# A chunk recurrence put on the diagonal corners of TensorE's array and scheduled first

## The chip, the cores and the metric

The kernel runs on one core of a Trainium2 chip. The metric is the device time of one execution in microseconds (us); three executions of the kernel before took 3286.41, 3289.52 and 3295.87 us, median 3289.52. The core has five engines that each work through a queue of their own in order: TensorE (PE in the profile; its weight loads are listed apart as PEld), VectorE (DVE), ScalarE (ACT), GpSimd (POOL) and SyncE (SP, which here issues DMAs).

## The reference

One decoder block on 2048 tokens of 1024 channels. A projection `w_in` feeds two mixers: eight heads of an RWKV-7 recurrence (64 channels each) and four heads of differential attention. Their outputs are concatenated, projected by `w_out`, added to the input, and followed by a gated MLP with a short causal convolution. The change touches the recurrence only:

```python
def step(state, inp):                       # per head, state is 64 x 64
    r_t, w_t, k_t, v_t, kk_t, a_t = inp
    sa = jnp.einsum('bhvk,bhk->bhv', state, -kk_t)
    state = (state * w_t[:, :, None, :]
             + sa[..., None] * (kk_t * a_t)[:, :, None, :]
             + v_t[..., None] * k_t[:, :, None, :])
    return state, jnp.einsum('bhvk,bhk->bhv', state, r_t)
_, y = lax.scan(step, s0, seq_major)        # 2048 steps
```

## The kernel before

The program is a list of instructions that a scheduler orders: each engine takes, of what is ready by the scheduler's own timing, the instruction that was written first, and buffers come from pools with a fixed number of slots per tag. So the order in which the Python code emits work is its priority.

The recurrence is done in 32 chunks of 64 tokens, two chunks to a group (16 groups, class `Rwkv`). For each group there are four steps. `prepare` (L383) makes the decayed keys and queries AR and BK for all eight heads (two heads per 128 partitions), multiplies them into the matrices M of each head (L470, tiles se and so for even and odd heads), transposes values into `sav` and keys into `bkt`, and sends the diagonal 32 x 32 blocks of M through DRAM (adr) into tile ab. `invert` (L502) inverts those blocks on VectorE by 31 pairs of dependent instructions (L515, L517) and sends the result X through DRAM (xdr) back into M, bdx and x1t, all by SP's queue. `join` (L535) makes the blocks off the diagonal. `scan` (L557) carries the state S over the two chunks:

- rp (L570, L573): what the old state and the chunk's own values give, for all heads, in PSUM partitions 0 to 63; ScalarE copies it to rsb (L575);
- sp (L578): rsb times the inverse, copied by ScalarE into the lower half of `sav` (L579);
- up (L583): the change of the state; VectorE adds it (L588) and applies the decay (L591), once for each half of the partitions;
- yp (L594, L597): the output, from the old state and from `sav`, added to ybv (L600).

The state is kept as 128 x 128 per pair of heads with zeros off the diagonal blocks. In `sav` the 64 upper partitions hold the values, the 64 lower ones the result of sp, for even and odd heads alike. A float32 matmul counts as two passes in the profile. `post` (L605) normalises and gates the last group's output in between.

`block_kernel` interleaves: first the blocks of the projection (tile pp, lines L99 to L101 in helper `mm3`, 24 matmuls for 512 tokens, in two halves of the tokens, the second named pp1_...), then the 64 attention units (4 heads of 16 query blocks; tiles sp at L775 to L778, tp at L813, op at L819, ot at L838) with the steps of the recurrence between them, at most up to unit 44 (`SPREAD`); from unit 40 (`ALONE`) attention uses the recurrence's PSUM slots. Then come the output projection (tile po) and the MLP (fp, dn). The recurrence's PSUM tiles have two slots in tag ra (prepare) and two in rc (join, scan, post).

Of the kernel before, what the change touches and what calls it, by code (L numbers as in the profile page):

```python
# [8 lines left out]
F32 = mybir.dt.float32  # L9
# [45 lines left out]
def rms_rstd(nc, cx, pool, src, n, eps, name, junk):  # L55
    """[128,1] = (mean(src^2) + eps)^-0.5 over the free axis; src is a list of APs."""
# [10 lines left out]
def norm_rows(nc, cx, pool, dst, src, gain, t):  # L67
    """dst = rms-normalised rows of src times gain; both SBUF [128, 1024], tokens x channels."""
# [9 lines left out]
def transpose_split(nc, cx, ps, xn, xh, xl, t, tag, bufs):  # L78
    """xn: SBUF [128, 1024] tokens x channels; writes tokens t*128.. of xh/xl, lists of [128, 8, GRP] tiles."""
# [16 lines left out]
def mm3(nc, out, lh, ll, rh, rl, n):  # L96
    """out = sum over kb of (lh+ll)^T (rh+rl) without ll*rl; callables give the operands of kb."""
# [28 lines left out]
class Proj:  # L126
    """Projections of x by w_in, one half of the tokens at a time."""
# [25 lines left out]
    def load(self, t, first=None):  # L153
        """128 tokens of normalised x, transposed and split; the second half's rows come from prepare()."""
# [38 lines left out]
    def pair(self, a, b, w=None):  # L193
        """Two blocks, the first tokens of both before the last."""
# [5 lines left out]
    def start(self, first):  # L200
        """Loads the first half and does its first two blocks."""
# [20 lines left out]
    def shift(self, cb, g, pp):  # L222
        """Token shift of an RWKV block."""
# [49 lines left out]
def rwkv_consts(tc, nc, cx, I):  # L273
# [95 lines left out]
class Rwkv:  # L369
    """Time mixing, 128 tokens at a time, in four stages per group."""  # L370
# [12 lines left out]
    def prepare(self, g):  # L383
# [71 lines left out]
        tt(BK[:, :, :, 0, :], c4(b2), c4(ip), op=ALU.mult)  # L455
        tt(BK[:, :, :, 1, :], c4(kp), c4(ip), op=ALU.mult)
# [697 lines left out]
```

## Time and profile before

| | |
|---|---|
| median of three runs | 3289.52 us |
| span of the profiled execution | 3295.9 us (the slowest run reads 3295.87 us, so nothing measurable lies around the span) |
| TensorE | 3178.5 us busy, 96% of the span |
| VectorE, ScalarE, GpSimd | 58%, 35%, 10% |
| granted TensorE clock, mean | 0.964 of full speed |
| chain that ended last | PE 82%, DVE 4%, DMA 4% |

Busy is the time in which an engine works on at least one instruction. The granted clock is a mean over two levels, 1.2 and 2.4 GHz, so 0.96 says that 8% of the time was spent at the lower one. By the tiles the span has four stages: projection with the first groups of the recurrence (to 943 us), attention with the rest of it (to about 1440), attention alone (to 1636), output projection and MLP (to the end).

### The profile page before, as it was taken

The page shows a single profiled execution, that of the slowest core. Times are in us where ns is not written, and L with a number is a line of the kernel's source. Part 1 is how long each engine was busy: PE and PEld are TensorE (multiplying, and loading weights), DVE is VectorE, ACT ScalarE, POOL GpSimd, SP SyncE. Part 2 cuts the span into 40 slices and gives each one's busy share as a digit, 9 for nine tenths or more (in the row PEclk, how much of TensorE's full clock was granted, in tenths as well). Part 3 has the DMA queues.
Part 4 walks back from the last instruction along what each step waited for, and adds up shares of the span by engine and source line. Part 5 has one row for each costly group of instructions (what it writes and reads, how often), then busy time and mean ns, then how long its engine had stood idle before and what let it go on. Part 6 is the DMA issues. An engine that isn't in the chain of part 4 may idle for free.

```text
span 3295.9 us, 44432 instructions
## 1 busy us (share of the span) xinstructions
PE 3178.5 (96%) x16579; PEld 2594.6 (79%) x16579; DVE 1923.8 (58%) x4898; ACT 1167.9 (35%) x2268; POOL 332.6 (10%) x441
## 2 busy tenths in 40 slices
PE   8999999999989989898999999999999999999997
PEld 6887777777777767677888888888888788888886
DVE  5246555455457868568655455555556655555556
ACT  4233322232225555467633422222223422222223
POOL 3001000010022232233200000000000000000002
PEclk9999999999878999899999999999999999999999
DMA  5355523234372252415244311111112411111112
GB/s 159 96 158 165 146 87 99 82 82 104 91 123 59 53 104 58 72 53 136 78 141 166 122 51 52 45 45 56 48 45 82 155 52 45 45 54 49 52 33 83
DMA packets 361177, 282.30 MB, mean 86 GB/s; under 512 B 95823, under 2 KB 307378, under 8 KB 360962
## 3 DMA queue, kind: packets, MB, share of 16 engines
q1 hardware_dynamic: 333874, 247.11, 25.9%
q0 software_dynamic: 24784, 28.16, 4.6%
q10 hardware_dynamic: 2304, 4.20, 0.4%
q8 instruction: 131, 2.15, 0.3%
q14 instruction: 84, 0.69, 0.1%
HBM read 204.72 MB, written 73.88 MB: 85 GB/s over the span
## 4 chain that ended last, share of the span: by engine, by line
PE 82%; DVE 4%; DMA 4%; issue 1%; ACT 1%; SPq 1%; POOL 0%; ACTq 0%; DVEq 0%; POOLq 0%
PE fp L99 10%; PE fp L101 9%; PE fp L100 9%; PE dn L100 5%; PE dn L99 5%; PE dn L101 5%; PE pp L99 4%; PE pp L100 4%; PE pp L101 4%; PE op L819 3%; PE po L99 2%; PE po L101 2%; PE sp L775 2%; PE po L100 2%; PE rp L573 2%; PE rp L570 2%
## 5 line engine op out<-in xcount | busy, mean ns | idle before, releaser
L1001 DVE TENSOR_TENSOR acc<-dn,acc 128x512 f32<-128x512 f32 x320 | 211.6, 688 | 224.3 <-PE dn L101 222.0
L99 PE MATMUL fp<-f1h,uh 128*128 128x512 f32 x704 | 275.8, 392 | 3.7 <-DVE fcarry L966 3.7
L100 PE MATMUL fp<-f1l,uh 128*128 128x512 f32 x704 | 275.2, 391 | 0.0
L101 PE MATMUL fp<-f1h,ul 128*128 128x512 f32 x704 | 275.1, 391 | 0.0
L100 PE MATMUL dn<-dl,gh 128*128 128x512 f32 x704 | 274.5, 390 | 0.0
L99 PE MATMUL fp<-f0h,uh 128*128 128x512 f32 x704 | 274.2, 389 | 0.0
L101 PE MATMUL fp<-f0h,ul 128*128 128x512 f32 x704 | 274.1, 389 | 0.0
L100 PE MATMUL fp<-f0l,uh 128*128 128x512 f32 x704 | 274.0, 389 | 0.0
L99 PE MATMUL dn<-dh,gh 128*128 128x512 f32 x704 | 271.7, 390 | 1.9 <-DVE acc L1001 1.9
L101 PE MATMUL dn<-dh,gl 128*128 128x512 f32 x704 | 263.4, 390 | 0.0
L780 DVE TENSOR_SCALAR_CACHE_REDUCE E<-sp 128x512 f32<-128x512 f32 (+3 forms) x320 | 188.4, 606 | 82.8 <-PE sp L778 45.7
L93 DVE TENSOR_TENSOR ul<-ur,uh 128x1024 fp32r<-128x1024 f32 x88 | 107.7, 1225 | 186.9 <-ACT uh L92 186.9
L962 DVE SCALAR_TENSOR_TENSOR u<-fp,cvA,u 128x511 f32<-128x511 f32 x176 | 131.4, 747 | 119.8 <-ACT u L960 119.8
L819 PE MATMUL op<-V,at 128*128 128x128 f32 x1088 | 163.6, 295 | 26.3 <-ACT at L815 25.3
L92 ACT CAST dh<-dr 128x1024 fp32r<-128x1024 f32 x44 | 44.4, 1047 | 386.6 <-PE dn L101 383.9
L819 PEld LDWEIGHTS op<-V,at 128*128 128x128 f32 x1088 | 146.1, 204 | 41.3 <-ACT at L815 32.7
L99 PE MATMUL pp<-x1h,wh 128*128 128x512 f32 x416 | 174.5, 419 | 0.0
L101 PE MATMUL pp<-x1h,wl 128*128 128x512 f32 x416 | 172.6, 415 | 0.0
L515 DVE TENSOR_TENSOR xtmp<-X,ab 128x60 f32<-128x60 f32 (+24 forms) x496 | 110.2, 222 | 105.9 <-DMA ab<-adr 76.2
L100 PE MATMUL pp<-x1l,wh 128*128 128x512 f32 x416 | 171.6, 412 | 0.0
L100 PE MATMUL pp<-x0l,wh 128*128 128x512 f32 x416 | 167.9, 404 | 0.0
L99 PE MATMUL pp<-x0h,wh 128*128 128x512 f32 x416 | 167.3, 403 | 0.1
(302 smaller groups left out, 7013.2 us busy)
## 6 DMA issues: line engine op xcount, KB each, us to landing
ur<-in_w_up SPq DMA_DIRECT2D x88, 512.0 KB
wr<-in_w_in SPq DMA_DIRECT2D x52, 512.0 KB
dr<-in_w_down SPq DMA_DIRECT2D x44, 512.0 KB
rw<-e SPq DMA_DIRECT2D x56, 256.0 KB
x<-in_x SPq DMA_DIRECT2D x16, 512.0 KB
qq<-e SPq DMA_DIRECT2D x64, 128.0 KB
kk<-e SPq DMA_DIRECT2D x64, 128.0 KB
ab<-adr SPq DMA_DIRECT2D x64, 128.0 KB
```

The source lines that it names most:

```text
L93: nc.vector.tensor_tensor(wl, wr, wh.bitcast(F32), op=ALU.subtract)
L99: nc.tensor.matmul(out, lh(kb), rh(kb), start=(kb == 0), stop=False)
L100: nc.tensor.matmul(out, lh(kb), rl(kb), start=False, stop=False)
L101: nc.tensor.matmul(out, ll(kb), rh(kb), start=False, stop=(kb == n - 1))
L515: tt(tv, X[:, 0:n, j:j + 1].broadcast_to([P, n, w]), ab[:, j:j + 1, j + 1:32].broadcast_to([P, n, w]), op=ALU.mult)
L570: nc.tensor.matmul(rp[0:64, 2 * hb:2 * hb + 2, :], AR[:, hb, c, 0, :], S[:, hb, :], start=True, stop=False)
L573: nc.tensor.matmul(rp[0:64, h, :], M[64:128, c, h, 0:64], sav[64:128, c, h, :], start=False, stop=(e == 1))
L775: nc.tensor.matmul(sp[:, 0:n], qa[:, c, qs], ka[:, c, 0:n], start=True, stop=False)
L780: nc.vector.tensor_scalar(e[ch * GRP // EW][:, eo:eo + n], sp[:, 0:n], -1.0, None, op0=ALU.mult, op1=ALU.min, accum_out=mx[:, ch:ch + 1])
L819: nc.tensor.matmul(op, at[:, q, :], v[:, q, :], start=(kb == 0), stop=(kb == qb))
L962: stt(u[:, 1:GRP], pp[:, 0:GRP - 1], w1(b), u[:, 1:GRP], op0=ALU.mult, op1=ALU.add)
L1001: nc.vector.tensor_tensor(acc[:, t, ds_], po, acc[:, t, ds_], op=ALU.add)
```

## The change

The even head of a pair now lives on partitions 0 to 63 and the odd head on 64 to 127 in everything that the recurrence reads: M, the two halves of `sav` and `bkt` change places for odd heads. The state shrinks to 64 columns per pair. rp, sp and the state's part of yp become eight matmuls each of 64 x 64 (rows 0 to 63 to columns 0 to 63 of the array for even heads, 64 to 127 to 64 to 127 for odd), even and odd in turn. The part of rp that comes from the chunk's own values is made in `prepare` (tile wp, copied to kv); VectorE adds rp to it. up and the other part of yp keep all 128 rows with 64 columns, even and odd in turn. The scan's instructions are emitted under `tc.high_priority()`, which puts them ahead of all else that is ready. The DMAs of adr and of M are split by even and odd heads. (Doc strings are removed as well; lines after them keep their places, later lines move.)

```diff
-        s = c.tile([P, 4, P], F32, name=f"state{i}")
+        s = c.tile([P, 4, 64], F32, name=f"state{i}")
...
-        tt(BK[:, :, :, 0, :], c4(b2), c4(ip), op=ALU.mult)
-        tt(BK[:, :, :, 1, :], c4(kp), c4(ip), op=ALU.mult)
+        for e in range(2):
+            rs = slice(64 * e, 64 * e + 64)
+            tt(BK[rs, :, :, e, :], c4(b2[rs]), c4(ip[rs]), op=ALU.mult)
+            tt(BK[rs, :, :, 1 - e, :], c4(kp[rs]), c4(ip[rs]), op=ALU.mult)
...
         for d in range(2):
-            ds_ = slice(32 * d, 32 * d + 32)
-            nc.sync.dma_start(adr[d].rearrange("b j i -> j b i"), M[ds_, :, :, ds_].rearrange("j c h i -> j (c h) i"))
+            for e in range(2):
+                r = 64 * e + 32 * d
+                nc.sync.dma_start(adr[d].rearrange("(b e) j i -> e j b i", e=2)[e],
+                                  M[r:r + 32, :, :, 32 * d:32 * d + 32].rearrange("j c (b e) i -> e j (c b) i", e=2)[e])
...
+        kv = T([P, NC, 4, 64], "kv", SB)
+        wp = U([P, NC, 4, 64], "wp")
+        for c in range(NC):
+            for hb in range(4):
+                for e in range(2):
+                    h, ks = 2 * hb + e, slice(64 * (1 - e), 64 * (1 - e) + 64)
+                    nc.tensor.matmul(wp[64 * e:64 * e + 64, c, hb, :], M[ks, c, h, 0:64], sav[ks, c, h, :],
+                                     start=True, stop=True)
+        nc.scalar.copy(kv, wp)
...
         for d in range(2):
-            ds_ = slice(32 * d, 32 * d + 32)
-            nc.sync.dma_start(M[ds_, :, :, ds_].rearrange("j c h i -> j (c h) i"),
-                              xdr[d].rearrange("b m s i -> (m s) b i"))
+            for e in range(2):
+                r = 64 * e + 32 * d
+                nc.sync.dma_start(M[r:r + 32, :, :, 32 * d:32 * d + 32].rearrange("j c (b e) i -> e j (c b) i", e=2)[e],
+                                  xdr[d].rearrange("(b e) m s i -> e (m s) b i", e=2)[e])
...
-            rp = U([P, 8, 64], f"rp{c}")
-            for hb in range(4):
-                nc.tensor.matmul(rp[0:64, 2 * hb:2 * hb + 2, :], AR[:, hb, c, 0, :], S[:, hb, :], start=True, stop=False)
+            with tc.high_priority():
+                rp = U([P, 4, 64], f"rp{c}")
+                for hb, e, h, rs in both:
+                    nc.tensor.matmul(rp[rs, hb, :], AR[rs, hb, c, 0, :], S[rs, hb, :], start=True, stop=True)
+                rsb = kv[:, c]
+                tt(rsb, rp, rsb, op=ALU.add)
+                sp = U([P, 4, 64], f"sp{c}")
+                for hb, e, h, rs in both:
+                    nc.tensor.matmul(sp[rs, hb, :], M[rs, c, h, 0:64], rsb[rs, hb, :], start=True, stop=True)
+                sv = sav[:, c].rearrange("p (b e) x -> e p b x", e=2)
                 for e in range(2):
-                    h = 2 * hb + e
-                    nc.tensor.matmul(rp[0:64, h, :], M[64:128, c, h, 0:64], sav[64:128, c, h, :], start=False, stop=(e == 1))
-            rsb = T([P, 8, 64], "rsb")
-            nc.scalar.copy(rsb[0:64], rp[0:64])
-            sp = U([P, 8, 64], f"sp{c}")
-            for h in range(8):
-                nc.tensor.matmul(sp[0:64, h, :], M[0:64, c, h, 0:64], rsb[0:64, h, :], start=True, stop=True)
-            nc.scalar.copy(sav[0:64, c], sp[0:64])
+                    rs = slice(64 * e, 64 * e + 64)
+                    nc.scalar.copy(sv[e][rs], sp[rs])
             next(post, None)
...
+            with tc.high_priority():
+                yp = U([P, 4, 64], f"yp{c}")
+                for hb, e, h, rs in both:
+                    nc.tensor.matmul(yp[rs, hb, :], S[rs, hb, :], AR[rs, hb, c, 1, :], start=(hb == 0), stop=False)
+                up = U([P, 4, 64], f"up{c}")
+                for hb, e, h, rs in both:
+                    nc.tensor.matmul(up[rs, hb, :], bkt[:, c, 64 * h:64 * h + 64], sav[:, c, h, :], start=True, stop=True)
+                st = T([P, 4, 64], "st")
+                tt(st, S, up, op=ALU.add)
+                tt(Sn, st, pc[:, :, c:c + 1].broadcast_to([P, 4, 64]), op=ALU.mult)
+                for hb, e, h, rs in both:
+                    nc.tensor.matmul(yp[rs, hb, :], sav[:, c, h, :], M[:, c, h, 64:128], start=False, stop=(hb == 3))
+                yv = ybv[:, :, 64 * c:64 * c + 64]
+                tt(yv, yp, yv, op=ALU.add)
```

The order of instructions moves with it. On TensorE, where the state is read for group 4's chunk 0 during the projection (rp0_4 is rp of chunk 0 of group 4, xp_4 its join, vt and bt group 5's transposes, pp the projection), there stood before:

```order
L101 MATMUL pp1_13_1_5090<-x1h1_3044,wl1_13_5055 128x512
L545 MATMUL xp_4_5223<-ident_84,x1t_4_5221 128x32 x4
L570 MATMUL rp0_4_5241<-state0_588,AR_4_4100 64x128
L573 MATMUL rp0_4_5241<-sav_4_4340,M_4_4305 64x64 x2
L570 MATMUL rp0_4_5241<-state0_588,AR_4_4100 64x128
L488 MATMUL vt_5_5123<-ident_84,vv_5_4875 128x128 x4
L496 MATMUL bt0_5_5131<-ident_84,BK_5_4883 128x128 x4
L573 MATMUL rp0_4_5241<-sav_4_4340,M_4_4305 64x64 x2
```

In the changed kernel (se1_5 and so1_5 are group 5's products, L590 is rp's new line, L560 the join's) there stands:

```order
L101 MATMUL pp1_13_1_5247<-x1h1_3129,wl1_13_5212 128x512
L560 MATMUL xp_4_5403<-ident_84,x1t_4_5401 128x32
L590 MATMUL rp0_4_5422<-state0_588,AR_4_4221 64x64 x8
L560 MATMUL xp_4_5403<-ident_84,x1t_4_5401 128x32 x3
L472 MATMUL se1_5_5185<-AR_5_5035,BK_5_5036 128x128 x2
L472 MATMUL so1_5_5186<-AR_5_5035,BK_5_5036 128x128 x2
```

The eight pieces of rp (five are shown), with other groups' work between them, have become one piece of eight equal matmuls.

At the end of the projection on TensorE (pp1_25_1 is its last tile) there stood before, from the last projection matmul on:

```order
L101 MATMUL pp1_25_1_7829<-x1h1_3044,wl1_25_7798 128x512
L470 MATMUL se0_10_7660<-AR_10_7522,BK_10_7523 128x128 x4
L545 MATMUL xp_9_7900<-ident_84,x1t_9_7793 128x32 x4
L570 MATMUL rp0_9_7939<-state0_588,AR_9_7026 64x128
L573 MATMUL rp0_9_7939<-sav_9_7188,M_9_7091 64x64 x2
```

In the changed kernel (up1_7 and gp_6 belong to the scan of group 7 and the post of group 6, n2_9 to the prepare of group 9):

```order
L101 MATMUL pp1_25_1_8169<-x1h1_3129,wl1_25_8138 128x512
L607 MATMUL up1_7_7266<-sav_7_6345,bkt_7_6355 64x64 x8
L644 MATMUL gp_6_7287<-sg_6_5630,gup_533 128x128 x4
L366 MATMUL n2_9_7322<-rT0_556,sel_555 128x128 x4
L560 MATMUL xp_8_7597<-ident_84,x1t_8_7595 128x32 x4
L590 MATMUL rp0_8_7688<-state0_588,AR_8_6769 64x64 x8
```

The first rp after the projection is that of group 9 before and that of group 8 now: one group more of the recurrence stands among the attention units. At the other end, the last rp (group 15, chunk 1) stood behind the output of head 2's query block 2 (unit 34) before, and stands behind that of its query block 7 (unit 39) now.

On SP's queue, among the attention units, the return of group 12's inverse (xdr_12) into M, bdx and x1t stood so before (ab_13 and X_13 are loads for the next group's inverse):

```order
L481 DMA ab_13_10221<-adr_13_10218 32x1024 x4
L483 DMA X_13_10226<-xinit_578 128x256
L523 DMA M_12_9278<-xdr_12_10382 32x16x32 x2
L528 DMA bdx_586<-xdr_12_10382 32x4x32 x4
L531 DMA x1t_12_10393<-xdr_12_10382 32x16x32
```

In the changed kernel:

```order
L485 DMA ab_13_10634<-adr_13_10629 32x1024 x4
L535 DMA xdr_12_10816<-X_12_9692 256x1x32 x4
L487 DMA X_13_10639<-xinit_578 128x256
L539 DMA M_12_9657<-xdr_12_10816 32x8x32 x4
L544 DMA bdx_586<-xdr_12_10816 32x4x32 x4
L547 DMA x1t_12_10829<-xdr_12_10816 32x16x32
```

The two issues of M are four of half the size (32x8x32 for 32x16x32), all ahead of the issue of x1t, and the four of xdr have moved between ab_13 and X_13.

## Rows read from the trace of the kernel before

**Rows 1.** Windows, PE alone, by stage; columns: stretch, length, busy (instructions), granted clock, DMA share, GB/s
```profile
160.00:943.00 783.00, 776.72 (x4448) 0.96 0.40 110
943.00:1440.00 497.00, 446.70 (x3097) 0.87 0.41 77
1440.00:1636.00 196.00, 174.03 (x1188) 0.97 0.37 91
1636.00:3296.00 1660.00, 1636.82 (x7232) 0.99 0.23 72
```

**Rows 2.** Timeline, PE, chunk 0 of group 3; columns: start, length, engine, line, operation, tiles, count
```profile
556.21 0.43 PE L570 MATMUL rp<-state,AR 128*64 128x128 f32 x2
556.57 0.44 PE L573 MATMUL rp<-sav,M 64*64 64x64 f32 x4
...
559.14 0.50 PE L99 MATMUL pp<-x1h,wh 128*128 128x512 f32 x1
...
574.69 1.14 PE L578 MATMUL sp<-rsb,M 64*64 64x64 f32 x16
575.76 1.13 PE L613 MATMUL mp<-ybv,ones 128*128 128x512 f32 x2
...
580.92 1.05 PE L583 MATMUL up<-sav,bkt 128*128 128x128 f32 x8
581.81 0.33 PE L594 MATMUL yp<-AR,state 128*128 128x64 f32 x2
582.07 0.34 PE L597 MATMUL yp<-M,sav 128*64 128x64 f32 x4
...
584.23 0.50 PE L99 MATMUL pp<-x1h,wh 128*128 128x512 f32 x1
```

**Rows 3.** Windows, line L470 alone, two stretches of TensorE at full clock
```profile
218.90:220.15 1.25, 1.16 (x16) 1.00 0.24 56
694.10:695.30 1.20, 1.11 (x8) 1.00 0.00 0
```

**Rows 4.** Windows, tile pp (projection) alone, four groups of recurrence
```profile
556.20:825.50 269.30, 154.08 (x563) 0.93 0.35 90
```

**Rows 5.** Windows, PE alone, during and after the rp of chunk 1, group 3
```profile
588.30:590.50 2.20, 2.20 (x19) 1.00 0.00 0
590.50:604.10 13.60, 13.60 (x56) 0.50 0.21 64
```

**Rows 6.** Waits of PE in 943 to 1440; columns: total us, times, longest
```profile
PE op L819 <- ACT at L815: 16.8, 8, 12.5
PE xp L545 <- DMA x1t<-xdr: 12.5, 2, 10.3
```

**Rows 7.** Timeline, all engines, the join of group 15
```profile
1388.44 0.84 SPq L523 DMA_DIRECT2D M<-xdr  x2
...
1394.03 0.64 PE L545 MATMUL xp<-ident,x1t 32*128 32x32 f32 x4 [10.33 <-DMA x1t<-xdr]
...
1394.60 0.69 PE L570 MATMUL rp<-state,AR 128*64 128x128 f32 x2
```

**Rows 8.** Timeline, PE: group 9's rp, the last yp, the fortieth attention unit's store
```profile
946.92 0.69 PE L570 MATMUL rp<-state,AR 128*64 128x128 f32 x2
...
1436.95 0.34 PE L597 MATMUL yp<-M,sav 128*64 128x64 f32 x4
...
1461.77 0.50 PE L838 MATMUL ot<-ident,on 128*128 128x128 f32 x3
```

**Rows 9.** Lines, 160 to 1450; columns: group, count, busy us, mean ns, idle before, releaser
```profile
L588 DVE TENSOR_TENSOR st<-state,up 64x256 f32<-64x256 f32 x64 | 26.6, 416 | 7.4 <-PE up L583 6.1
L455 DVE TENSOR_TENSOR BK<-t_e,t_d 128x512 f32<-128x512 f32 x16 | 12.1, 758 | 0.2
L575 ACT COPY rsb<-rp 64x512 f32<-64x512 f32 x32 | 18.5, 578 | 52.9 <-PE rp L573 52.5
```

**Rows 10.** Tile rp, what ended the idle time before its instructions; columns: us, times
```profile
  PE rp L573: 52.5, 22
```

More of the change, by code (lines that the diff above doesn't have):

```diff
@@ L489, in prepare @@
         for q in range(2):
-            nc.scalar.copy(sav[64:128, q].rearrange("p h x -> p (h x)"),
-                           vt[64 * q:64 * q + 64].rearrange("p h x -> p (h x)"))
+            for e in range(2):
+                nc.scalar.copy(sav[64 * (1 - e):64 * (1 - e) + 64, q].rearrange("p (b e) x -> e p b x", e=2)[e],
+                               vt[64 * q:64 * q + 64, :, 64 * e:64 * e + 64])
         bkt = T([P, NC, 512], "bkt", SB)
@@ L509, in invert @@
             qs = slice(32 * q, 32 * q + 32)
[L510 removed]
+            r = 64 * (q % 2)
+            nc.sync.dma_start(cx.bda[qs, :, qs], mq[r:r + 32, :, q, 32:64])
         tmp = T([P, 8 * 16], "xtmp")
@@ L521, in invert @@
         for d in range(2):
-            ds_ = slice(32 * d, 32 * d + 32)
-            nc.sync.dma_start(M[ds_, :, :, ds_].rearrange("j c h i -> j (c h) i"),
-                              xdr[d].rearrange("b m s i -> (m s) b i"))
+            for e in range(2):
+                r = 64 * e + 32 * d
+                nc.sync.dma_start(M[r:r + 32, :, :, 32 * d:32 * d + 32].rearrange("j c (b e) i -> e j (c b) i", e=2)[e],
+                                  xdr[d].rearrange("(b e) m s i -> e (m s) b i", e=2)[e])
         xq = xdr[1].rearrange("(t q) m s i -> q (m s) t i", q=4)
@@ L553, in join @@
             nc.tensor.matmul(bank[0:32, t, :], t1[:, t, :], cx.bdx[:, t, :], start=True, stop=True)
-        nc.scalar.copy(mv[0:32, :, 32:64], bank[0:32].rearrange("p t (q i) -> p (t q) i", q=4))
+        mv = M.rearrange("p c (b e) x -> e p (c b) x", e=2)
+        bv = bank[0:32].rearrange("p t (b e i) -> e p (t b) i", b=2, e=2)
+        for e in range(2):
+            nc.scalar.copy(mv[e][64 * e:64 * e + 32, :, 32:64], bv[e])
         yield
@@ L563, in scan @@
         L = self.live[g]
-        AR, M, sav, bkt, ybv, pc = (L[n] for n in ("AR", "M", "sav", "bkt", "ybv", "pc"))
+        AR, M, sav, bkt, ybv, pc, kv = (L[n] for n in ("AR", "M", "sav", "bkt", "ybv", "pc", "kv"))
+        both = [(hb, e, 2 * hb + e, slice(64 * e, 64 * e + 64)) for hb in range(4) for e in range(2)]
         for c in range(NC):
-            S, Sn = cx.S[cx.scur], cx.S[1 - cx.scur]
-            cx.scur = 1 - cx.scur
-            rp = U([P, 8, 64], f"rp{c}")
-            for hb in range(4):
-                nc.tensor.matmul(rp[0:64, 2 * hb:2 * hb + 2, :], AR[:, hb, c, 0, :], S[:, hb, :], start=True, stop=False)
-                for e in range(2):
-                    h = 2 * hb + e
-                    nc.tensor.matmul(rp[0:64, h, :], M[64:128, c, h, 0:64], sav[64:128, c, h, :], start=False, stop=(e == 1))
-            rsb = T([P, 8, 64], "rsb")
-            nc.scalar.copy(rsb[0:64], rp[0:64])
-            sp = U([P, 8, 64], f"sp{c}")
-            for h in range(8):
-                nc.tensor.matmul(sp[0:64, h, :], M[0:64, c, h, 0:64], rsb[0:64, h, :], start=True, stop=True)
-            nc.scalar.copy(sav[0:64, c], sp[0:64])
-            next(post, None)
-            up = U([P, 4, P], f"up{c}")
-            for hb in range(4):
-                nc.tensor.matmul(up[:, hb, :], bkt[:, c, hb * P:(hb + 1) * P], sav[:, c, 2 * hb:2 * hb + 2, :],
-                                 start=True, stop=True)
-            st = T([P, 4, 64], "st")
-            for e in range(2):
-                rs = slice(64 * e, 64 * e + 64)
-                tt(st[rs], S[rs, :, rs], up[rs, :, rs], op=ALU.add)
-            for e in range(2):
-                rs = slice(64 * e, 64 * e + 64)
-                tt(Sn[rs, :, rs], st[rs], pc[rs, :, c:c + 1].broadcast_to([64, 4, 64]), op=ALU.mult)
-            yp = U([P, 4, 64], f"yp{c}")
-            for hb in range(4):
-                nc.tensor.matmul(yp[:, hb, :], S[:, hb, :], AR[:, hb, c, 1, :], start=True, stop=False)
-                for e in range(2):
-                    h = 2 * hb + e
-                    nc.tensor.matmul(yp[64 * e:64 * e + 64, hb, :], sav[:, c, h, :], M[:, c, h, 64:128],
-                                     start=False, stop=True)
-            yv = ybv[:, :, 64 * c:64 * c + 64]
-            tt(yv, yp, yv, op=ALU.add)
```

8 lines of the change are left out of this document (4 added, 4 removed).

## The prediction, made before the changed kernel was run

> **What bounds the kernel now.** I read the windows by stage first. Up to 943 us, where the projection runs beside the first groups of the recurrence, TensorE is busy for 776.7 of 783 us; among the attention units it is busy for 446.7 of 497 us [rows 1]. So in the first stage every microsecond that TensorE gives up ends the stage that much earlier, if what it executes is shorter and not only its bookkeeping. In the second it does so only while the other engines and the DMAs keep up: 50.3 us there are waits, the longest for the DMA that brings x1t and for ScalarE's copies [rows 6]. The last two stages contain nothing of the change. I then read the granted clock: 0.96 in the first stage and 0.87 in the second [rows 1], which is 31 us and 65 us lost against full clock (0.04 of 783, 0.13 of 497). One drop shows what goes before it: rp of chunk 1 of group 3 still began at full clock (1.00 up to 590.5), and for the 13.6 us behind it the clock was 0.50, the lower of its two levels, although TensorE was never idle [rows 5]. Last I read one undisturbed chunk in the timeline, which gives the prices.
>
> **What a chunk costs TensorE before.** From start to start of the next work [rows 2]: rp 559.14 - 556.21 = 2.93 us, sp 575.76 - 574.69 = 1.07, up 581.81 - 580.92 = 0.89, yp 584.23 - 581.81 = 2.42; together 7.3 us, and 234 us in 32 chunks. rp is the dear one: 24 passes at 0.122 us, where the 16 passes of sp, all in one corner of the array, take 0.067 each. It changes eight times between all rows and a corner; its surplus over sp, 24 x 0.055 = 1.3 us, is 0.16 us a change.
>
> **What a chunk costs TensorE after.** The diff gives six packs of 16 passes with 64 columns of weights and 64 of data: wp, rp, sp, the state's part of yp, up, the rest of yp. That is 96 passes for 72, so the gain hangs on the price of a pass, which the trace of before does not show for the diagonal corners. Upper bound: a pack costs what sp costs, 1.07 us, and a chunk 6.4 us. Lower bound: the two corners work side by side and nothing is added, 0.53 us a pack, 3.2 us a chunk. The nearest row is L470, whose even and odd heads use different row halves: where they alternate, 16 matmul passes were busy for 1.16 us, where one half ran alone, 8 took 1.11 [rows 3]. Side by side two halves cost the time of one. So I take half of sp, 0.53, and for the some four changes of shape that are left in a chunk 4 x 0.16, or 0.11 a pack (an estimate from rp's surplus): 0.65 us a pack, 3.9 us a chunk. The gain is 3.4 us a chunk, 109 us in all.
>
> On the Trainium skill: "TensorEngine Tiling (Array Packing)", section "Restrictions and Gotchas", says that different row tiles can't access the same PSUM bank at the same time. se and so have a PSUM tile each, so no row here tests it, while even and odd heads of the new rp share one tile on different partitions. If the rule holds for that too, the side-by-side gain is lost for the corner packs; that is the second rival below.
>
> **Edits beside TensorE.** VectorE: one add and one decay instead of two each, 0.42 us less apiece, the rp addition 0.42 more, and two more BK products of 0.76 us a group [rows 9]: some 0.3 us more a chunk, 10 us in all on an engine that is busy for 58% of the span; covered in the first stage by TensorE's projection. ScalarE: no rsb copy (0.58 us), against halved copies and one copy of kv a group, which are not in the trace; from nothing saved to 0.6 us either way a chunk, covered likewise; I take 0. SP: two more issues for adr and two for M each group, at 0.84 / 2 = 0.42 us [rows 7], so x1t, which stands behind them, is issued 1.7 us later. In the first stage the projection hides it; in the second TensorE has already been seen waiting 10.33 us for x1t [rows 7], so I count it in full. The priority itself: the order shows rp as one piece, but the recurrence is not ahead of where it was. At the end of the projection it is a whole group behind, because the projection's blocks have closed up.
>
> **The sum.** First stage: before, the scans of groups 0 to 8 lie in it, 18 x 7.3 = 131 us; after, those of groups 0 to 7, 16 x 3.9 = 62. The other work of the group that moves out: in four groups 269.3 - 154.1 = 115.2 us were not projection, 28.8 a group [rows 4]; less two chunks (14.6) and about 2 of half-clock time, 12 us. Together 69 + 12 = 81. Of the 31 us lost to the clock I take half back, as the burst of rp is a fifth of its length and the other sparse bursts stay: 15. The stage ends 96 us earlier, at 847.
>
> Second stage: scans 14 x 7.3 = 102 before, 16 x 3.9 = 62 after: -40; the group's other work +12; its share of waits and clock, (50 + 65) / 7 = +16; SP's issues 8 x 1.7 = +13. Sum +1. So nearly the whole gain is that of the first stage, and the attention stages last as long as before with one group more in them. 3295.9 - 96 + 1 = 3201 us for the profiled execution. This one was the slowest of three, 6.4 us over the median; against the median of 3289.5 the forecast is 3195 us.
>
> **The rivals.**
>
> *The chain keeps its pace.* In the second stage a group took (1394.60 - 946.92) / 6 = 74.6 us [rows 7, 8]. If that is the length of the dependent chain (products, DMA, inverse, DMA, join, scan) and not TensorE's load, TensorE's savings turn into waits there. Group 8 reads the state at 847, group 15 seven periods later at 1369, the last yp comes 42 us after that [rows 7, 8], at 1411; the recurrence now ends at about the fortieth unit, from whose store the second and third stage had 1636 - 1462 = 174 us left [rows 8]: 1585, and 1598 with SP's 13 us. That is 38 us before 1636: 3252 against the median. For it: the waits on x1t. Against it: TensorE was the busier one, at a lower clock.
>
> *The corners do not overlap.* Then wp, rp, sp and the state's part of yp cost 1.07 each, the column-split packs 0.65: 5.6 us a chunk. First stage 131 - 90 + 12 = 53, clock 8; second stage 102 - 90 - 12 - 29 = -29. Sum 32 us less: 3257. For it: nothing shows two corners writing one PSUM tile. Against it: L470.
>
> *Slower: the scan's wait moves to VectorE.* ScalarE stood idle for rp 52.5 us in 22 waits, 2.4 us each [rows 9, 10]. The addition that takes its place is on VectorE, in whose queue the inverse's 62 dependent instructions and attention's reductions stand behind it. Two such waits a group (4.8 us), two more BK products (1.5) and SP's issues (1.7) make the period 74.6 + 8.0 = 82.6 us. The point from which it decides: the stage ends where it did when the period is (1636 - 174 - 42 - 847) / 7 = 81.9 us. At 84 us the kernel is 7 x 2.1 = 15 us slower: 3305. Against it: rp holds TensorE for 0.65 us in place of 2.93, so what VectorE waits for comes sooner.
>
> **How the numbers follow.** The forecast has 0.57, its own range being 3130 to 3235: the lower bound of a pack gives 22 us more, a clock that stays high in both stages some 45 more, the upper half of a pack's price 40 less. The chain's pace has 0.19, corners that do not overlap 0.14, the slower case 0.10. Less than 0.3%, some 10 us, can't be told from no change. The first three cases are faster by more than that unless the two small ones slip by three quarters: faster 0.85, the same 0.06, slower 0.09. For the range I go from 3130 to 3270, which holds most of the chain and corner cases and leaves out the slower one and the tail of a wholly restored clock.
>
> **What would show it.** In the profile after: the first rp behind the projection near 847; rp, sp and both yp with pairs of matmuls that start within some 10 ns, a pack in 0.5 to 0.8 us; a clock above 0.97 in the first stage; the last yp near 1367 and the output projection from 1541. Packs of 1.07 us mean the second rival; a group period that stays at 74 us with longer waits of TensorE the first; VectorE idle for rp, with a period over 82, the third. I am wrong altogether if the first stage does not shorten, since it rests on TensorE's own time alone.

## The result and the profile after

The changed kernel took 3171.45 us (median of four executions, 3163.65 to 3178.39), beside 3292.69 us for the kernel before on the same chip: a ratio of 0.963, 95% interval 0.9595 to 0.9664, 121 us less. The forecast was 3195 us, with a range from 3130 to 3270. Run a second time, the changed kernel gave 3176.51 us and 0.9628 (0.959 to 0.9665).

The profiled execution took 3163.65 us. It is the shortest of its four, and the profiled one of before (3295.87 us) was among the longer, so the two lie 134 us apart where the medians lie 121. First its windows by stage, TensorE alone (columns as in [rows 1]; the stages are cut where the projection, the recurrence and the attention end):

```profile
160.00:828.00 668.00, 656.24 (x4576) 0.99 0.46 127
828.00:1327.00 499.00, 437.73 (x3878) 0.90 0.42 84
1327.00:1502.00 175.00, 152.35 (x1051) 0.91 0.37 93
1502.00:3162.00 1660.00, 1637.47 (x7232) 0.99 0.23 72
```

The first stage lasts 668 us instead of 783, at a clock of 0.99 instead of 0.96. Recurrence with attention last 499 instead of 497, attention alone 175 instead of 196, and the last stage has not moved. So 115 of the 134 us between the two profiled executions come out of the first stage.

The timeline of TensorE for chunk 0 of group 3 (columns as in [rows 2]) has the new packs:

```profile
544.83 0.68 PE L590 MATMUL rp<-state,AR 64*64 64x64 f32 x16
545.44 0.37 PE L560 MATMUL xp<-ident,x1t 32*128 32x32 f32 x3
...
562.92 0.68 PE L595 MATMUL sp<-kv,M 64*64 64x64 f32 x16
563.53 1.12 PE L627 MATMUL mp<-ybv,ones 128*128 128x512 f32 x2
...
568.78 0.68 PE L604 MATMUL yp<-AR,state 64*64 64x64 f32 x16
569.39 0.69 PE L607 MATMUL up<-sav,bkt 128*64 128x64 f32 x16
569.91 0.64 PE L612 MATMUL yp<-M,sav 128*64 128x64 f32 x16
570.48 0.51 PE L100 MATMUL pp<-x1l,wh 128*128 128x512 f32 x1
```

From start to start of what follows, rp takes 545.44 - 544.83 = 0.61 us where it took 2.93, sp 0.61 (1.07), the two parts of yp 0.61 and 0.57 (2.42 together), up 0.52 (0.89). Within such a pack the starts of the sixteen passes alternate by 6 to 7 ns and by 52 ns: even and odd head start as a pair, and a pair follows a pair after 58 ns. In sp of before, where all passes use one corner, the starts lie 58 ns apart too, one pass at a time. So eight steps of 58 ns have taken the place of sixteen, and some 0.14 us at the ends of a pack stay as they were (1.07 - 16 x 0.058 before, 0.61 - 8 x 0.058 now). wp, at 34 ns a pass, adds 0.54 us a chunk. That is 3.46 us at full clock, for 7.3 before.

Where the stages end, again from TensorE's timeline (group 8's rp, group 15's, the last yp, the first matmul of the out-projection; compare [rows 8]):

```profile
831.17 0.68 PE L590 MATMUL rp<-state,AR 64*64 64x64 f32 x16
...
1299.31 1.12 PE L590 MATMUL rp<-state,AR 64*64 64x64 f32 x16
...
1325.95 0.69 PE L612 MATMUL yp<-M,sav 128*64 128x64 f32 x16
...
1501.88 0.79 PE L99 MATMUL po<-woh,mh 128*128 128x512 f32 x1 [1.79 <-ACT mh L92]
```

A group takes (1299.31 - 831.17) / 7 = 66.9 us behind the projection, where it took 74.6 [rows 7, 8]. What TensorE waits for there, 828 to 1327 (columns as in [rows 6]):

```profile
PE op L833 <- ACT at L829: 25.0, 19, 7.2
PE xp L560 <- DMA x1t<-xdr: 8.9, 4, 4.5
```

Both waits of before are still there, neither is the scan's. Last, the two lines of tile rp that answer to [rows 10]: VectorE, now the engine that takes rp over (count; shortest, median and longest in ns; first and last start in us), and how long it sat idle for it (us, times).

```profile
L592 DVE TENSOR_TENSOR kv<-rp,kv x32: 402/418/425, 292.8 to 1322.4; 128x256 f32<-128x256 f32 x32
...
  PE rp L590: 19.5, 11
```

To see which term was worth what, I added up TensorE's time from the start of each matmul to the start of the next, by kind of work (gaps over 1.2 us count as waiting, less 0.3 us for the matmul itself; "half" is the part of the work, without the waiting, that fell into stretches at a granted clock of 0.5; the last row is the changed kernel's second profile, "again" below):

| us | scan | projection | group's other work | attention | waiting | sum | half |
|---|---|---|---|---|---|---|---|
| stage 1, before | 137.6 | 487.2 | 152.3 | | 6.0 | 783 | 64.9 |
| stage 1, after | 57.2 | 475.8 | 125.1 | | 10.3 | 668 | 15.8 |
| stages 2 and 3, before | 117.5 | | 109.1 | 409.1 | 57.5 | 693 | 114.5 |
| stages 2 and 3, after | 62.3 | | 133.2 | 417.7 | 60.8 | 674 | 110.6 |
| stages 2 and 3, again | 63.6 | | 134.9 | 422.6 | 65.6 | 687 | 138.2 |

### The profile page after: what moved, and what is told of

It is laid out like the page before. It is cut to its first block, busy times and chain, and to the rows that moved or that the text cites. A ratio compares the mean times of both kernels' runs of the same rounds, so it can differ in the third digit from the quotient of the medians.

```text
span 3161.9 us, 46143 instructions
## 1 busy us (share of the span) xinstructions
PE 3027.9 (96%) x17347; PEld 2489.9 (79%) x17347; DVE 1912.3 (60%) x4898; ACT 1168.6 (37%) x2332; POOL 328.2 (10%) x441
## 4 chain that ended last, share of the span: by engine, by line
PE 78%; DVE 6%; DMA 3%; ACT 1%; issue 1%; SPq 1%; POOL 0%; DVEq 0%; ACTq 0%; POOLq 0%
PE fp L99 10%; PE fp L101 10%; PE fp L100 10%; PE dn L100 5%; PE dn L99 5%; PE dn L101 5%; PE pp L100 4%; PE pp L99 4%; PE pp L101 4%; PE op L833 3%; PE po L99 2%; PE po L101 2%; PE po L100 2%; PE sp L789 1%; PE sp L790 1%
## 5 line engine op out<-in xcount | busy, mean ns | idle before, releaser
L803 ACT ACTIVATE E<-E,asc 128x1024 f32<-128x1024 f32 (+7 forms) x160 | 153.6, 963 | 37.1 <-DVE asc L799 36.6
L101 PE MATMUL pp<-x0h,wl 128*128 128x512 f32 x416 | 167.0, 402 | 0.0
```

What stands on the lines that cost most here:

```text
L101: nc.tensor.matmul(out, ll(kb), rh(kb), start=False, stop=(kb == n - 1))
L803: nc.scalar.activation(e[i][:, 0:n], e[i][:, 0:n], AF.Exp, bias=nm, scale=-1.0, accum_out=z)
```

## The experiments

The theory: the gain is TensorE's own time in the packs (fewer changes of shape, and two corners at work side by side), and it counts in full in the first stage. Its rivals: the priority makes it by shortening the chain; the corners do not overlap. Ratios are to the kernel before, run on the same chip; those of the changed kernel itself are 0.963 and 0.9628.

| kernel | us | ratio, 95% interval | projection ends | out-projection starts |
|---|---|---|---|---|
| before | 3292.69 | 1 | 943 | 1636 |
| after | 3171.45 | 0.963, 0.9595 to 0.9664 | 828 | 1502 |
| again (the same) | 3176.51 | 0.9628, 0.959 to 0.9665 | 830 | 1517 |
| grouped | 3242.88 | 0.986, 0.984 to 0.9879 | 886 | 1584 |
| serial | 3202.30 | 0.9736, 0.971 to 0.9762 | 866 | 1539 |
| prionly | 3263.30 | 0.9924, 0.9894 to 0.9954 | 894 | 1599 |
| nopri | 3193.78 | 0.9709, 0.9682 to 0.9735 | 836 | 1533 |
| prirp | 3170.49 | 0.9624, 0.9606 to 0.9643 | 839 | 1503 |
| x1tfirst | 3188.97 | 0.9662, 0.9634 to 0.969 | 847 | 1539 |
| spread45 | 3174.37 | 0.9626, 0.9595 to 0.9658 | 829 | 1514 |
| cvearly | 3187.77 | 0.9668, 0.9638 to 0.9699 | 845 | 1527 |
| cvearly_s48 | 3173.73 | 0.9625, 0.9588 to 0.9662 | 842 | 1513 |
| cvlate | 3177.88 | 0.9645, 0.9624 to 0.9665 | 829 | 1513 |
| cvlate_s48 | 3150.44 | 0.9566, 0.9548 to 0.9583 | 828 | 1494 |

**grouped: the changes of shape alone.** The kernel before, with rp and the two parts of yp each in one sweep:

```diff
             for hb in range(4):
-                nc.tensor.matmul(rp[0:64, 2 * hb:2 * hb + 2, :], AR[:, hb, c, 0, :], S[:, hb, :], start=True, stop=False)
-                for e in range(2):
-                    h = 2 * hb + e
-                    nc.tensor.matmul(rp[0:64, h, :], M[64:128, c, h, 0:64], sav[64:128, c, h, :], start=False, stop=(e == 1))
+                nc.tensor.matmul(rp[0:64, 2 * hb:2 * hb + 2, :], AR[:, hb, c, 0, :], S[:, hb, :], start=(hb == 0), stop=False)
+            for h in range(8):
+                nc.tensor.matmul(rp[0:64, h, :], M[64:128, c, h, 0:64], sav[64:128, c, h, :], start=False, stop=(h == 7))
```

> The kernel before with the same passes for rp and yp, but all passes over all rows first and then all those of one corner or half, so one change of shape in place of eight in each. My theory (0.16 us for a change of shape, read from rp's surplus over sp): rp goes from 2.93 to about 1.8 us and yp from 2.42 to about 1.7, 1.8 us a chunk; 18 chunks of the first stage are 33 us, the second stage gives back a part: 3240 to 3265 us. Rival (shape changes cost nothing and the passes over all rows are dear in themselves): rp stays at 2.9 us and the time within 10 us of the kernel before, 3283 to 3303 us.

Timeline of TensorE, rp of chunk 0 of group 3 in grouped:

```profile
548.81 0.93 PE L570 MATMUL rp<-state,AR 128*64 128x128 f32 x7
549.66 1.14 PE L572 MATMUL rp<-sav,M 64*64 64x64 f32 x16
550.74 0.50 PE L99 MATMUL pp<-x1h,wh 128*128 128x512 f32 x1
```

rp takes 550.74 - 548.81 = 1.93 us and not 2.93, with the same 24 passes and 6 changes fewer: 0.17 us a change, as rp's surplus over sp had said. yp came to 1.55 us from 2.42 in the same chunk. The ratio is a gain of 1.4%, 44 us by the medians, in the expected band: the first theory stands on this point. In its profile the scans took 46 us less at full clock; 20 us that the lower clock no longer cost and 16 us of new waiting nearly cancel.

**serial: one corner after the other.** The changed kernel, every pack with its four even heads ahead of its four odd ones:

```diff
-        both = [(hb, e, 2 * hb + e, slice(64 * e, 64 * e + 64)) for hb in range(4) for e in range(2)]
+        both = [(hb, e, 2 * hb + e, slice(64 * e, 64 * e + 64)) for e in range(2) for hb in range(4)]
```

(and the same two loops exchanged for wp).

> The changed kernel with all even heads of a pack ahead of all odd ones, so that consecutive passes use the same corner (the same passes, in another order). My theory (two corners work side by side, a pack in 0.61 us): a pack takes what sp took before, some 1.07 us, 0.46 us more; six packs a chunk and 32 chunks are 88 us, of which the first stage's share of 18 packs in 36 (16 chunks, 44 us) counts in full and the second stage's in good part: 3230 to 3265 us. Rival (the gain is the smaller number of shape changes, and the order of heads doesn't matter): packs stay at 0.6 to 0.7 us and the time within 10 us of the changed kernel, 3165 to 3185 us.

Timeline, rp of chunk 0 of group 3 in serial, and what follows it:

```profile
552.91 0.96 PE L590 MATMUL rp<-state,AR 64*64 64x64 f32 x16
553.80 0.37 PE L560 MATMUL xp<-ident,x1t 32*128 32x32 f32 x3
```

The windows by stage of serial, TensorE alone:

```profile
160.00:866.00 706.00, 693.75 (x4644) 0.98 0.44 120
866.00:1341.00 475.00, 425.36 (x3678) 0.91 0.44 85
1341.00:1539.00 198.00, 174.52 (x1183) 0.94 0.36 89
```

A pack takes 0.89 us and not 0.61, so the corners do overlap, and that rival falls. By the ratios (0.9736 to 0.963) what the run takes away is worth some 35 us; the rival of this run, that the order of heads does not matter, falls too. But the run does not take all of the overlap away. In each pack of serial that stands by itself three passes of the odd heads still start within 4 to 6 ns of a pass of the even ones, where the corner changes; the rest follow one another at 58 ns, as in sp of before. Between two packs it shows in the timeline (odd heads of up, even heads of yp, from the scan of the same chunk):

```profile
578.65 0.27 PE L612 MATMUL yp<-M,sav 128*64 128x64 f32 x1
578.71 0.22 PE L607 MATMUL up<-sav,bkt 128*64 128x64 f32 x1
578.76 0.22 PE L612 MATMUL yp<-M,sav 128*64 128x64 f32 x1
578.77 0.22 PE L607 MATMUL up<-sav,bkt 128*64 128x64 f32 x1
578.82 0.22 PE L612 MATMUL yp<-M,sav 128*64 128x64 f32 x1
578.82 0.22 PE L607 MATMUL up<-sav,bkt 128*64 128x64 f32 x1
```

Three pairs that overlap save 3 x 0.058 = 0.17 us, which is what lies between sp's 1.07 and the 0.89 here. So a pass in one corner costs the same in both layouts, five of eight pairs were taken apart and not eight, and that is in the main why the run came out at 3202 and not in 3230 to 3265. Start to start, all 32 scans grew from 120 to 167 us, and the profiled execution by 36 us, with 5 us less time at half clock: some three quarters of what TensorE spends more is paid.

**prionly and nopri: the priority.** prionly is the kernel before with the two parts of its scan, cut as in the changed kernel, under the highest priority (the first of the two places):

```diff
-            S, Sn = cx.S[cx.scur], cx.S[1 - cx.scur]
+            with tc.high_priority():
+                S, Sn = cx.S[cx.scur], cx.S[1 - cx.scur]
```

nopri is the changed kernel without it, in both places:

```diff
-            with tc.high_priority():
+            if True:
```

> The kernel before with its recurrence's instructions at the highest priority, and nothing else changed. My theory (the packs make the gain): within 0.3% of the kernel before, 3283 to 3303 us, the half-clock time stays near its 236 us. Rival (the priority makes a good part of the 121 us): 3230 to 3260 us, with a group period under 70 us in the second stage.

> The changed kernel without the highest priority: the recurrence's instructions are handed to the scheduler like all others. My theory (the gain is TensorE's own time in the packs): no difference beyond 0.3%, 3165 to 3185 us, since the first stage's end rests on what TensorE executes and not on its order; the period of a group in the second stage stays near the 66.9 us of the changed kernel. Rival (the priority shortens the chain): the period of a group goes back towards the 74.6 us of before, which over seven groups is 54 us, so about 3225 us, with longer waits of TensorE among the attention units.

Both bands of my theory were missed: the priority is worth 0.8% in the kernel before and some 0.8% in the changed one, against none expected. Beside the same runs of the kernel before, the packs without the priority (nopri) save 93 us and the priority without the packs (prionly) 23; together that is 116 of the 121. The rival's mechanism, a shorter period by the priority, can't be told from these runs: in prionly a group behind the projection takes (1363.42 - 895.67) / 7 = 66.8 us, under 70 as the rival had it (its time, 3263 us, lies just outside the rival's 3230 to 3260), but in nopri it takes (1307.6 - 834.2) / 7 = 67.6. So the period falls with either edit alone, and the priority is not what keeps it short in the changed kernel. What stands out in nopri is one wait. TensorE's waits there, 836 to 1330:

```profile
PE sp L595 <- DVE kv L592: 16.1, 1, 16.1
PE op L833 <- ACT at L829: 14.9, 14, 2.0
```

And the timeline of VectorE in nopri, where it happens (in square brackets the idle time before, and what ended it):

```profile
849.16 1.27 DVE L434 TENSOR_TENSOR_SCAN t_d<-sgate,t_b 128x256 f32<-128x256 f32 x2
867.76 0.19 DVE L530 TENSOR_TENSOR xtmp<-X,ab 128x31 f32<-128x31 f32 x1 [17.33 <-DMA ab<-adr]
...
868.32 0.42 DVE L592 TENSOR_TENSOR kv<-rp,kv 128x256 f32<-128x256 f32 x1
```

rp was done by 850.6 us, but VectorE's queue had the first step of an inverse ahead of rp's addition, and that waited 17.33 us for its DMA; sp stood behind the addition, and attention behind sp. In the changed kernel TensorE's sp waits for that addition 1.1 us in all between 160 and 1330 us:

```profile
PE sp L595 <- DVE kv L592: 1.1, 2, 0.5
```

The sums of stages 2 and 3 agree in part: nopri 697 us to 674, of which waiting is 77.6 to 60.8, 17 of the 23 us, with one chunk less in these stages. But the work at half clock is 149 us there for 111, which is 19 us lost, in part right behind that wait (854 to 878 us) and in part far behind it (1086 to 1202). What share of this belongs to the missing priority stays open.

In prionly the first stage ends at 894 instead of 943: it holds 16 chunks and not 18 (scan 120.0 us for 137.6, the group's other work 127.0 for 152.3), and 27 us at half clock for 64.9. The stages behind take the moved work for 12 us more than before (705 to 693). Over the three stages the only thing that fell is the time at half clock, 110 us for 179; half of that difference is 35 us, near the 38 by which its profiled execution is shorter. How much of this another execution would repeat, one profile does not say (see "again"). The windows of its first stage, and of the one long drop of the clock in it:

```profile
160.00:894.00 734.00, 726.36 (x4203) 0.98 0.42 115
591.40:611.80 20.40, 20.40 (x78) 0.50 0.18 56
```

**prirp: which part of the priority.** The changed kernel with the priority on rp, the addition, sp and its copies alone:

```diff
             next(post, None)
-            with tc.high_priority():
+            if True:
                 yp = U([P, 4, 64], f"yp{c}")
```

> The changed kernel with the highest priority only for the first part of a chunk (rp, VectorE's addition, sp, the copies into sav) and not for the state and the output. My theory (what the priority is worth is the place of the addition in VectorE's queue, whose wait of 16.1 us stood in the kernel without the priority): TensorE waits nowhere for the addition by more than 4 us, and the time is that of the changed kernel within 10 us, 3162 to 3182 us. Rival (the priority of the state's update, on which the next chunk hangs, makes the 22 us): 3185 to 3200 us.

0.9624, the changed kernel's own ratio, and TensorE waits 0.8 us for the addition between 160 and 1330 us:

```profile
PE sp L595 <- DVE kv L592: 0.8, 1, 0.8
```

So the priority of this first part is enough, and that of the state's update adds nothing that this shows. That it works by the addition's place in VectorE's queue fits the wait that is gone; no run gave the priority to the addition alone.

**x1tfirst: SP's issues in the way of x1t.** The DMAs for x1t and bdx ahead of the four into M:

```diff
+        x1t = T([P, 16, 32], "x1t")
+        nc.sync.dma_start(x1t[0:32], xdr[0].rearrange("b m s i -> (m s) b i"))
+        L["x1t"] = x1t
+        xq = xdr[1].rearrange("(t q) m s i -> q (m s) t i", q=4)
+        for q in range(4):
+            qs = slice(32 * q, 32 * q + 32)
+            nc.sync.dma_start(cx.bdx[qs, :, qs], xq[q])
         for d in range(2):
             for e in range(2):
...
-            nc.sync.dma_start(cx.bdx[qs, :, qs], xq[q])
...
-        nc.sync.dma_start(x1t[0:32], xdr[0].rearrange("b m s i -> (m s) b i"))
```

> The changed kernel with the DMAs for x1t and for the block diagonal of the second inverse issued ahead of the four that write the inverse into M; nothing else is moved. My theory (SP's issues stand in the way of x1t, 1.7 us a group from the two added ones): x1t lands some 3 us earlier in each group, TensorE's wait for x1t (8.9 us in four waits in the second stage) gets shorter, 5 to 15 us less in all: 3156 to 3167 us. Rival (the wait is covered, or another one takes its place at the next link, the write into M that sp reads): within 5 us of the changed kernel, 3166 to 3177 us.

TensorE's waits in x1tfirst, 847 to 1333:

```profile
PE op L832 <- ACT at L828: 19.5, 10, 8.6
PE vp L751 <- DMA vtl<-vT: 8.7, 1, 8.7
...
PE xp L559 <- DMA x1t<-xdr: 3.5, 3, 1.8
```

And its second stage, TensorE alone:

```profile
847.00:1333.00 486.00, 425.13 (x3566) 0.81 0.43 80
```

The wait for x1t fell from 8.9 us to 3.5 as expected, and nothing was won: 0.9662, if anything slower than the changed kernel. A wait of 8.7 us for attention's values, which is not among the longer ones of the changed kernel, stands there now, and the clock of the second stage was 0.81 for 0.90: up to the out-projection some 208 us of work at half clock in place of 126, 41 us lost, where the profiled execution is 36 us longer. What pulled the clock down stays open; waits and order changed together, so the run shows that the shorter wait brought no gain, not what it would bring at the same clock.

**again and spread45: what moves without a cause.** The changed kernel untouched, and with one number of the order changed (`SPREAD` 45 for 44).

> The changed kernel a second time, nothing altered, for a second profile. If the clock follows from the order of the work (my theory of why the small variants differ): the half-clock time between the projection and the out-projection is again near 137 us and the same long waits of TensorE stand in the same places (17 us or so either way), 3163 to 3180 us. Rival (the half-clock time is chance from one execution to the next, and with it the 20 us by which the variants differ): the half-clock time moves by 40 us or more, and the time with it by 20.

> The changed kernel with the recurrence's steps spread over 45 attention units instead of 44, a number that takes away or adds no work: it only re-sorts the order behind the projection. It shows how far the time moves by order alone. My theory: the first stage ends within 3 us of 828, and the time within 25 us either way of the changed kernel, 3150 to 3196 us, by waits and half-clock time in the attention stages. Rival (the order among the attention units is worth nothing, and the 22 us without the priority are the priority's own): within 8 us, 3163 to 3180 us.

The first two stages of the second profile of the changed kernel:

```profile
160.00:830.00 670.00, 657.44 (x4572) 0.98 0.46 126
830.00:1341.00 511.00, 448.42 (x3875) 0.88 0.41 82
```

Its long waits of TensorE behind the projection (828 to 1520):

```profile
PE cvB_ps L48 <- DMA cvB_st<-in_conv_b: 8.9, 1, 8.9
PE xp L560 <- DMA x1t<-xdr: 8.6, 4, 4.3
```

The same order with the same long waits (8.9 us for the table of the convolution, 8.1 in the first profile; 8.6 for x1t, 8.9 there) lasted 15 us longer than in the first profile, and its work at half clock in stages 2 and 3 is 138 us for 111, which is 14 us lost; waiting in all is 66 us for 61. So the clock is not a function of the order alone; it moves one kernel by some 15 us from one execution to the next. The eight executions of the two runs lie between 3162.62 and 3180.14 us. My theory and its rival were both half right: the waits repeat, the clock does not. spread45, at 3174 us, lies in its rival's narrow band too: a re-sorted order need not cost anything. One run of it doesn't bound what another order can do.

**cvearly, cvlate, with 44 or 48 units: a better version.** In the changed kernel TensorE waits 8.1 us at the end of the recurrence for the DMA of a table, and 27 us at half clock follow. cvearly loads and transposes the two tables ahead of the recurrence; cvlate only moves their transposes behind the loads of `w_out`; _s48 sets SPREAD to 48. In cvlate each table is also loaded through a buffer of its own. The diff is that of cvlate_s48 (in cvearly both lines of the tables stand behind `attn_consts`):

```diff
-    st = pool.tile([P, P], F32, name=f"{name}_st", tag="tab_st")
+    st = pool.tile([P, P], F32, name=f"{name}_st", tag=f"{name}_st")
...
-        ctA = load_table(nc, cx, tmp, nc.sync, [cw[0], cw[1]], "cvA")()
-        ctB = load_table(nc, cx, tmp, nc.sync, [cw[2], cb], "cvB")()
+        tabs = [load_table(nc, cx, tmp, nc.sync, [cw[0], cw[1]], "cvA"),
+                load_table(nc, cx, tmp, nc.sync, [cw[2], cb], "cvB")]
         for kb in range(KB):
...
+        ctA, ctB = (f() for f in tabs)
...
-PER, PER2, SPREAD = 1.5, 3.5, 44
+PER, PER2, SPREAD = 1.5, 3.5, 48
```

> The changed kernel with the convolution's two tables loaded and transposed before the recurrence starts, instead of when it ends. My theory: TensorE's 8.4 us wait for the table's DMA goes, and with it the 27 us at half clock behind it (13 us lost): 15 to 20 us less, 3150 to 3158 us, unless the re-sorted order brings another wait. Rival (the wait is replaced by the one for ScalarE's copies that stands beside it, and the clock falls anyway): within 8 us of the changed kernel.

> As the last, and with the recurrence's steps spread over 48 attention units instead of 44, so that less attention is left to run alone behind the recurrence. My theory (attention alone keeps TensorE at 87 per cent, and its waits are for ScalarE): a few units fewer stand alone, 5 to 15 us less than with the tables moved alone, 3140 to 3155 us. Rival (the recurrence's chain, 67 us a group, is the limit and not the order given to it): no difference to the tables moved alone beyond 10 us.

> The changed kernel with the transposes of the convolution's two tables behind the loads of the out-projection's weights instead of ahead of them; their DMAs are issued where they were. My theory: TensorE's wait of 8.1 to 8.9 us for the table goes, with the 24 to 27 us at half clock behind it (12 to 13 us lost): 15 to 20 us less, 3150 to 3160 us. Rival (in this stretch ScalarE's copies for attention are the limit, so the wait only moves): within 6 us of the changed kernel, 3166 to 3180 us.

> As the last, and with the recurrence's steps spread over 48 attention units instead of 44. Moving from 44 to 48 shortened the stages behind the projection from 682 to 670 us in the pair with the tables moved to the front. My theory (less attention alone behind the recurrence): 8 to 14 us less than with the tables alone, 3138 to 3152 us. Rival (that difference was the re-sorted order's own): between 3145 and 3175 us, no better than the tables alone.

The tables alone bring nothing either way. In cvearly TensorE waits for both tables at the start of the kernel:

```profile
PE cvB_ps L48 <- DMA cvB_st<-in_conv_b: 7.4, 1, 7.4
PE cvA_ps L48 <- DMA cvA_st<-in_conv_w: 5.3, 1, 5.3
```

and the first stage ends 17 us later. In cvlate the wait is gone, but the clock falls to half near the same place (24 us from 1373 us on, 27 from 1359 in the changed kernel), attention alone takes 180 us all the same, and waiting in stages 2 and 3 is 67 us in all, not less than the 61 of the changed kernel: the rival was right. With 48 units the windows of cvlate_s48 are

```profile
160.00:828.00 668.00, 653.37 (x4572) 0.99 0.46 126
828.00:1349.00 521.00, 464.02 (x4007) 0.89 0.40 82
1349.00:1494.00 145.00, 129.62 (x924) 0.94 0.44 107
```

so the recurrence ends 22 us later and attention alone is 30 us shorter; waiting is 52 us. The kernel takes 3150.44 us, 0.9566 of before (0.9548 to 0.9583), some 20 us better than the changed kernel, with intervals that do not meet. Both pairs gained with 48 (14 and 27 us); what the later transposes add to it I did not run by itself.

## Why the prediction was right, and where it was not

**The first stage bounded by TensorE's own time: right.** It shortened by 115 us, forecast 96. By the table above: scans at full clock 132.4 us before (137.6 less half of the 10.5 at half clock) and 56.6 after, 76 us for the 69 forecast, since a chunk costs 3.46 us and not 3.9; the group's other work 20 us for 12; the clock (64.9 - 15.8) / 2 = 24.5 us for 15; waiting 4 us more, which I had not counted. The term most mis-sized in this stage is the clock: I took half of the loss back and three quarters came; three short drops are left before 828 us. My reason for it, the rp burst ahead of a drop [rows 5], covers only a part. prionly keeps rp as it was, and that very drop stands in it again (0.50 from 591.40 to 611.80), while neither grouped nor the changed kernel has it; but the six drops of before that came behind it (some 41 us) are gone in prionly too, and its first stage had a clock of 0.98. What made those stays open.

**Half of sp as the price of a pack, 0.53 plus 0.11: right.** 0.61 us for three of them, 0.52 to 0.57 for the others. The way there holds too: two halves side by side cost the time of one, in eight steps of 58 ns for sp's sixteen, and 0.14 us at the ends is near a change of shape. The price of 0.16 us a change of shape was confirmed by grouped at 0.17. The Trainium skill, "TensorEngine Tiling (Array Packing)", section "Key Properties", says that a change of the tiling mode drains the engine; grouped, with its 0.17 us a change, agrees.

**Corners that do not overlap: wrong.** Packs take 0.61 us, serial's 0.89 with three of eight pairs left, and 1.07 was the price of none. The rule of the Trainium skill on which I had weighed it, in the same page's "Restrictions and Gotchas" (different row tiles can't access one PSUM bank at the same time), does not hold back the diagonal pairs of this kernel: rp's even and odd heads write one tile on different partitions, and their passes start 6 to 7 ns apart.

**Stages 2 and 3, forecast +1, measured -19 in one profile and -6 in the other: the step that failed.** The forecast held the attention stages at their old length with one group more in them, by +16 for waits and clock of an extra group and +13 for SP's issues. At full clock (each kind of work less half of its time at half clock) the scans saved 45 us there for the 40 forecast, and the group's other work cost 25 and 23 more and not 12. The +13 did not come: TensorE waited 8.9 and 8.6 us for x1t, not longer than the 12.5 of before [rows 6], and x1tfirst shortened that wait and won nothing. The +16 is not settled by these runs: waits and clock together came to +1 us in the first profile and to +20 in the second, with the same order of work.

Over all three stages the sum is plainer than I made it. The scans fell from 255 to 120 us and the profiled execution by 134 (119 in the second profile); the projection (-11), the group's other work (-3), attention (+9) and waiting (+8) nearly cancel. That the total came so near is in part luck. The packs without the priority saved 93 us (nopri), and my sum for them was 95, though its terms for the two attention stages were off both ways; the 24 us that the forecast lacked are about what the priority brings, which I had put at nothing.

**The chain keeps its 74.6 us: wrong,** it went to 66.9, and the waiting in stages 2 and 3 grew by 3 and 8 us, not by the 55 that the scans saved there. **The scan's wait moves to VectorE: the mechanism is real, the price was not.** I had seen that the addition would stand in VectorE's queue behind the inverse. Without the priority it did, once, for 16.1 us, but in one group and not as two small waits in each. My price for this case did not hang together either: 3305 was reckoned from 84 us a group, where its own sum gave 82.6, 5 us slower and not 15. And I had costed the priority at nothing, by the order alone; it is worth some 0.8%, 26 us, of which that wait is 16. The first stage's end does move little without it (836 for 828, with one chunk more in it).

**What would show it:** first rp behind the projection 831.17 (near 847 forecast), pairs within 10 ns, packs of 0.5 to 0.6 us, clock 0.99 in the first stage, last yp 1325.95 (1367), out-projection from 1501.88 (1541). VectorE's idle time for rp fell to 19.5 us where ScalarE had 52.5.

## What to carry to other kernels

Price a small matmul by its start-to-start time in an undisturbed stretch, and look for what its neighbours add: here the changes of shape alone were worth 1.4%, with the same passes. Where one engine is the busiest in every stage, sum what it saves over all of them, and add a new wait only when a queue shows who would cause it. When a step moves to another engine, read what stands in that engine's queue and what that waits for; one addition behind a DMA wait cost 16 us in one place, and a priority on that step and its neighbours took it back. And when a run is meant to take an effect away, count in its trace how much of the effect is left: serial kept three of eight pairs.

## What the runs showed of the hardware that was not expected

Sixteen float32 passes of 64 x 64 took 0.61 us with even and odd corner in turn and 0.89 us with one corner after the other, although both write one PSUM tile. One corner starts such a pass every 58 ns, the two diagonal corners a pair of them every 58 ns, and up and the second part of yp, which use all rows and one half of the columns each, start in the same pairs. Even with one corner after the other, three passes of the second corner started within 6 ns of one of the first. And one program with the same order and the same long waits spent 111 us of its work in stages 2 and 3 at half clock in one execution and 138 in another.
